# A retention layer's first head: loads in a chain, stores on another queue, sample updates between the two halves of the state

## The chip, the core and the metric

The kernel runs on one core of one Trainium2 chip. The metric is the device time of one launch in microseconds (us). Engines have these names in the profile: PE (matrix products), ACT and DVE (elementwise work), POOL, and SP, which here only issues transfers (DMA). ACT and POOL issue transfers as well. Each engine works through its own queue of instructions in order, and waits at an instruction until the semaphores that it names have been raised.

## The reference, cut to what matters

One inference step of a decoder of two layers: a short gated convolution with its feed-forward part, then a retention layer with its feed-forward part, for 512 prompt tokens and 8 x 4 sample tokens that go on from a stored state. D = 1024, 4 heads, 256 columns of q and k and 512 of v a head. What the change touches is the retention layer:

```python
z = x @ w_in                                     # q, k, v, g of all heads
q = rotary(q, pos); k = rotary(k, pos) * (HEAD_DK ** -0.5)
# per head, in chunks (prompt) or in one step on the stored state s0 (sample):
scores = einsum('bhid,bhjd->bhij', qc, kc) * decay
inner  = einsum('bhij,bhjv->bhiv', scores, vc)
cross  = einsum('bhid,bhdv->bhiv', qc, S) * cross_w
S_new  = S * chunk_decay + einsum('bhjd,bhjv->bhdv', kc * state_w, vc)
# o = inner + cross, normalized per head, times silu(g), then @ w_out
```

The outputs include the new states of prompt and samples. All arithmetic is float32.

## The kernel before

Every product is done in three passes of a reduced float32 type: each operand is split into a high part (rounded, by ACT) and a low part (the rest, by DVE: `split`, L186-188), and high x high, high x low and low x high are summed (`mm3`, `project`, and in the value products L814, L815, L816). So each weight piece is loaded (`load_piece`, L134), split and multiplied. A piece can also be split "adding" (`split_adding`, L189-196): ACT writes the high part and its negative into the place of the low part, and a DMA issued by POOL (L195) adds the weight from memory to it. That spares DVE a pass and costs a transfer that adds.

A scheduler puts instructions into the queues of the engines by the order of the program and by due times; `tc.issue_after(ins)` only keeps an instruction behind `ins` in the same queue. It does not wait for `ins` to be done. Buffers come in turns from pools: a tile that takes the place of others waits for all who still use them.

The retention layer begins inside the feed-forward part of layer 0. `ahead` (L846) makes the q and k of head 0 (L864 scales them, L866 stores them to `qk_made`), the v of head 0 (`value_products(0, ...)`, with `first` None, whose third and fourth weight pieces are loaded inside the loop at L827) and the gates of heads 0 to 2, in six `Job`s (products at L460; `gates`, L888; the store at L906). All of it goes to memory and is loaded again by each head.

Then the heads are walked through in a loop (L1289). For a head but the last:
- `value_products(h + 1, ...)` makes the next head's values from four weight pieces, c0 to c3; L821 is the sample tokens' product with the raw piece. Around the pieces, `first()` calls `value_loaded` (loads `vw` and `vsw`), and `then(c)` loads sample states and makes operands: S0 and S1 after piece 0, S2 and `operands_made` (transposes of k, L1069) after piece 1, `value_sample` after piece 2. For head 0, the loads and rotations of q and k (`qk_loaded`, L971; `gt` is the table of gains, L964; the rotations are L980 and L1011-1016) stand before it.
- `sample_operands`, `value_out` (stores the next head's values), `state(h, 0)` and `state(h, 1)`: the prompt's state after two and four chunks, the first split into `mid` (L187/188).
- `scores` of both halves, then `sample_outputs(0)` (L1231, L1233: the samples' q times the stored state S0), `states_update(0)` (L1249, and on DVE L1254, then the store of S0) and the load of S3 into the place of S0.
- `inner` of four blocks with the other sample outputs and updates between them, the next head's q and k, and `out_project`.

The last head has no next head: two pieces of its gate (`gate_project`) take the place of the values. Their order is written out: `operands_made`, gate 0, `value_sample`, S2, `sample_operands`, `state(0)`, gate 1, `state(1)`.

Of the kernel before, what the change touches and what calls it, by code (L numbers as in the profile page):

```python
# [12 lines left out]
P = 128  # L13
# [6 lines left out]
T = SEQ + NS  # L20
# [28 lines left out]
def hybrid_decode_kernel(ctx: ExitStack, tc: tile.TileContext, a: dict, o: dict):  # L49
# [7 lines left out]
    def nm(s):  # L57
        uid[0] += 1
        return f"{s}_{uid[0]}"
# [71 lines left out]
    def parts2(n, pool=None, tags=("wh", "wl")):  # L131
        return [(pool or wts).tile([P, n], F32R, tag=t, name=nm(t)) for t in tags]

    def load_piece(src, n, parts=False, sw=None, keep=None, adding=False):  # L134

        if sw is None:
            w = wts.tile([P, n], F32, tag="w", name=nm("w"))
            wh, wl = parts2(n)
        else:
            w = sw.tile([P, n], F32, tag="w2", name=nm("w2"))  # L140
            wh, wl = parts2(n, sw, ("h2", "l2"))

        def load(c=slice(0, n), queue=nc.sync):
            last_load[0] = queue.dma_start(w[:, c], src[:, c])

        def parted(c=slice(0, n)):
            if adding:
                return split_adding(wh, wl, w, src)
            return split(wh[:, c], wl[:, c], w[:, c])

        if keep is not None:
            keep.append(w)
        if parts:
            return wh, wl, load, parted
        load()
        parted()
        return wh, wl
# [632 lines left out]
    v_made = [dram.tile([P, 5, DV], F32, tag=f"v{h}", name=nm("vm")) for h in range(NH)]  # L790
    gate_made = [dram.tile([P, 4, T], F32, tag=f"g{h}", name=nm("gm")) for h in range(AHEAD)]

    def value_piece(h, c, raw, adding=False):
        return load_piece(a["rtv"][h, c], 2 * DV, keep=raw, adding=adding)

    def value_products(h, xs, first=None, then=None, ws=None):

        pv = [bank() for _ in range(4)]
        pvs = psum()
        if ws is None:  # L800
            raw = []
            ws = [value_piece(h, c, raw, first is None) for c in range(2)]
        else:
            ws, raw = ws
        if first is not None:
            first()
        for c in range(4):
            wh, wl = ws[c]
            for k2 in range(2):
                kt = 2 * c + k2  # L810
                cw = slice(k2 * DV, (k2 + 1) * DV)
                for tt in range(4):
                    ts_, out = slice(tt * P, (tt + 1) * P), pv[tt]
                    nc.tensor.matmul(out, xh[kt][:, ts_], wh[:, cw], start=(kt == 0), stop=False)  # L814
                    nc.tensor.matmul(out, xh[kt][:, ts_], wl[:, cw], start=False, stop=False)  # L815
                    nc.tensor.matmul(out, xl[kt][:, ts_], wh[:, cw], start=False, stop=(kt == KT - 1))  # L816
            if c % 2:

                for g in range(4):
                    kt = 2 * c - 2 + g  # L820
                    nc.tensor.matmul(  # L821
                        pvs[g * NS : (g + 1) * NS, 0, :], xs[:, kt, :],
                        raw[kt // 2][:, kt % 2 * DV : (kt % 2 + 1) * DV],
                        start=(c == 1), stop=(c == 3), skip_group_check=True,
                    )
            if c < 2:
                ws.append(value_piece(h, c + 2, raw, first is None))  # L827
            if then is not None:
                then(c)
        return pv, pvs  # L830
# [15 lines left out]
    def ahead(tp, fp, sw, one):  # L846
# [16 lines left out]
        def off(which, dt, pt):  # L863
            each(lambda p, d, r: nc.vector.tensor_mul(d, p, r), pt, halves(made[which][:, dt, :]), R)  # L864
            if dt:
                nc.gpsimd.dma_start(qk_made[which], made[which])  # L866

        off(1, 0, pts[0])
        off(1, 1, pts[1])
# [18 lines left out]
        def gates(h, n):  # L888
            made = {}

            def tile2():
                if not made:
                    made[0] = tp.tile([P, 2, T], F32, tag="gu", name=nm("gate"))
                return made[0]

            def gate(what, src):
                g = tile2()
                if what == "c21":
                    nc.scalar.activation(g[:, 1, :HT], src, AF.Silu)
                elif what == "c22":  # L900
                    nc.scalar.activation(g[:, 1, HT:], g[:, 1, HT:], AF.Silu)
                elif what == "c12":
                    nc.scalar.activation(g[:, 0, :], g[:, 0, :], AF.Silu)
                    for i in range(2):
                        nc.scalar.activation(g[:, i, :], g[:, i, :], AF.Copy, scale=g_ret(h * 4 + n + i))
                    nc.scalar.dma_start(gate_made[h][:, n : n + 2, :], g)  # L906

            return Job([a["rtg"][h, n + i] for i in range(2)], oh, ol, sw, summed(tile2, gate))
# [11 lines left out]
    with ExitStack() as c2:  # L920
# [49 lines left out]

        def qk_loaded(st):  # L971

            for which in (1, 0):
                nc.sync.dma_start(st["rot"][which], qk_made[which])
                if which:
                    for i, t in enumerate((cos, sin)):
                        nc.sync.dma_start(t, a["rope"][i])
            for which in (1, 0):
                r = st["rot"][which]
                nc.vector.tensor_mul(r, r, st["gt"][:, which, :].unsqueeze(1).to_broadcast([P, 2, T]))  # L980
                rotate(st, which)
# [43 lines left out]
        def value_loaded(h, st):  # L1025
# [1 line left out]
            vw = tp.tile([P, 4, T], F32, tag="gate", name=nm("vw"), bufs=1)[:, :, :DV]  # L1027
            vsw = tp.tile([P, DV], F32, tag="yn", name=nm("vsw"))
            nc.sync.dma_start(vw, v_made[h][:, 0:4, :])
            nc.sync.dma_start(vsw, v_made[h][:, 4, :])  # L1030
            vh = tp.tile([P, 4, DV], F32R, tag="vyh", name=nm("vh"), bufs=1)
            vl = tp.tile([P, 4, DV], F32R, tag="vyl", name=nm("vl"), bufs=1)
            for i in range(2):
# [186 lines left out]
        def states_load(h, st, i):  # L1220
            r, dt = RD[i]
            S = st["S"][i] = sp.tile([P, 4, DV], F32, tag="S", name=nm("S"))
            nc.sync.dma_start(S, rets_in[r, h, dt])
# [33 lines left out]
        def out_project(h, st, rest=None):  # L1257
# [27 lines left out]
                        residual(n, pts[n])  # L1285
            wide("m")

        st = qk_start(0)
        qk_loaded(st)  # L1289
        for h in range(NH):  # L1290
# [2 lines left out]

            def first():
                value_loaded(h, st)

            def then(c):
                if c == 0:
                    for i in range(2):
                        states_load(h, st, i)  # L1300
                elif c == 1:
                    states_load(h, st, 2)
                    operands_made(h, st)
                elif c == 2:
                    value_sample(h, st)

            if more:
# [6 lines left out]
                outs = [None, (slice(0, 2), va), (2, vb[0]), (3, vb[1]), (4, vc)]  # L1314
                value_out(h + 1, pv, pvs, list(zip(rows, outs)))
                state(h, st, 0)
                state(h, st, 1)
            else:
                gw = load_piece(a["rtg"][h, 0], KT * P)
                first()  # L1320
                for i in range(2):
                    states_load(h, st, i)
                operands_made(h, st)
                gate_project(h, st, 0, ws=gw)
                value_sample(h, st)
                states_load(h, st, 2)
                sample_operands(h, st)
                state(h, st, 0)
                gate_project(h, st, 1)
                state(h, st, 1)  # L1330
            for c in range(2):
                scores(h, st, c)
            sample_outputs(h, st, 0)
            states_update(h, st, 0)
            states_load(h, st, 3)
            yn0 = normalized(inner(h, st, 0))
            sample_outputs(h, st, 1)
            yn1 = normalized(inner(h, st, 1))
# [165 lines left out]
```

## Time and profile before

| | |
|---|---|
| median of 3 runs | 1494.57 us (1493.96 to 1496.03) |
| the profiled execution | 1492.83 us, span 1491.0 us |
| granted clock of PE, mean | 0.991 |
| PE busy | 1458.5 us (98%), 10944 products |
| DVE, ACT, POOL busy | 960.0, 612.1, 90.8 us |
| the six gate jobs' products (L460) | 635.98 to about 700 us |
| first L821 in the pass of head 0, 1, 2 | 710.68, 828.93, 930.29 us |
| first L1207 in the pass of the last head | 1021.83 us |

Times in the trace are counted from the span's start. The profiled execution is 1.8 us longer than its span, and 1.7 us shorter than the median. The clock column of a stretch is the share of full speed that PE was granted; a wait line names PE's tile and line, who ended the wait, the total in us, how often, and the longest. In a timeline line, the last bracket is the engine's idle time before the instruction and who ended it. A DMA line's own time is only that of issuing; the landing is a time of its own.

### The profile page before, as it was taken

Reading aid. Unit: us, or ns where it says so; the run is one execution under the profiler, and the core shown is the slowest. Engines: PE = TensorE matmul, PEld = TensorE weight load, DVE = VectorE, ACT = ScalarE, POOL = GpSimd, SP = SyncE. Lnnn points to the kernel's source line nnn. Section 1 sums busy time; section 2 is a strip of 40 time slices with the busy share of each in tenths; the row PEclk is TensorE's granted clock in tenths of the full one; section 3 lists DMA queues with packets and bytes.
Section 4 is the critical chain, followed back from the end, with each engine's and each line's share of the span. In section 5 each row is a group of like instructions: output and inputs, shape, how many; then the busy total and the mean of one; then the engine's idle time right before and its main releaser. Section 6 shows DMA issues by size and latency. Waiting matters only on the chain.

```text
span 1491.0 us, 26121 instructions
## 1 busy us (share of the span) xinstructions
PE 1458.5 (98%) x10944; PEld 1382.4 (93%) x10944; DVE 960.0 (64%) x1465; ACT 612.1 (41%) x883; POOL 90.8 (6%) x115
## 2 busy tenths in 40 slices
PE   9999999999999999899799999999999999999998
PEld 9999999999999999699479789788799999999997
DVE  6554439848658556675677485594759857848645
ACT  5222365525435335465323312323255625525424
POOL 1000220000000003000000000000030000000002
PEclk9999999999999999899899999999999999999999
DMA  6222273322222316544755573672545232222322
GB/s 222 86 86 86 95 177 106 103 89 100 89 96 96 103 47 167 161 147 156 282 200 184 175 259 122 209 257 72 198 127 128 88 107 90 97 89 100 99 65 82
DMA packets 77591, 195.40 MB, mean 131 GB/s; under 512 B 7184, under 2 KB 24464, under 8 KB 77088
## 3 DMA queue, kind: packets, MB, share of 16 engines
q1 hardware_dynamic: 69984, 171.71, 34.3%
q0 software_dynamic: 3344, 12.20, 4.5%
q10 hardware_dynamic: 4144, 9.81, 1.7%
q8 instruction: 86, 1.41, 0.4%
q14 instruction: 33, 0.27, 0.1%
HBM read 162.82 MB, written 30.88 MB: 130 GB/s over the span
## 4 chain that ended last, share of the span: by engine, by line
PE 88%; DVE 5%; issue 3%; DMA 2%; ACT 1%; POOL 1%; SPq 0%; DVEq 0%; ACTq 0%; POOLq 0%
PE mm L174 35%; PE sm L460 30%; PE sm L174 12%; PE sm L815 2%; PE sm L816 1%; PE sm L814 1%; PE sm L162 1%; DVE S L1254 1%; PE sm L164 1%; PE sm L163 1%; PE sm L1233 1%; DVE wl L188 1%; DMA S<-in_rets_dram 1%; DMA wl<-in_rtv_dram 1%; DVE xl L200 0%
## 5 line engine op out<-in xcount | busy, mean ns | idle before, releaser
L187 ACT ACTIVATE wh<-w 128x1024 fp32r<-128x1024 f32 (+4 forms) x209 | 203.9, 978 | 408.7 <-PE mm L174 204.4
L188 DVE TENSOR_TENSOR wl<-w,wh 128x1024 fp32r<-128x1024 f32 (+4 forms) x209 | 235.8, 1131 | 45.0 <-ACT wh L187 42.8
L460 PE MATMUL sm<-oh,wh 128*128 128x272 f32 x672 | 194.3, 289 | 0.0
L460 PE MATMUL sm<-oh,wl 128*128 128x272 f32 x672 | 194.2, 289 | 0.0
L460 PE MATMUL sm<-ol,wh 128*128 128x272 f32 x672 | 193.9, 289 | 0.0
L174 PE MATMUL mm<-xh,wh 128*128 128x272 f32 x868 | 182.3, 291 | 0.5 <-ACT wh L187 0.3
L174 PE MATMUL mm<-xh,wl 128*128 128x272 f32 x868 | 179.5, 289 | 0.0
L174 PE MATMUL mm<-xl,wh 128*128 128x272 f32 x868 | 178.8, 287 | 0.0
L268 DVE TENSOR_TENSOR x<-x,mm 128x544 f32<-128x544 f32 x85 | 61.2, 720 | 143.5 <-PE mm L174 143.4
L460 PE MATMUL sm<-oh,l 128*128 128x272 f32 x504 | 145.7, 289 | 0.0
L460 PE MATMUL sm<-oh,h 128*128 128x272 f32 x504 | 145.5, 289 | 0.0
L460 PE MATMUL sm<-ol,h 128*128 128x272 f32 x504 | 145.5, 289 | 0.0
L174 PEld LDWEIGHTS mm<-xh,wh 128*128 128x128 f32 x868 | 135.5, 188 | 2.5 <-ACT oh L187 0.8
L174 PEld LDWEIGHTS mm<-xl,wh 128*128 128x128 f32 x868 | 135.9, 188 | 0.1
L174 PEld LDWEIGHTS mm<-xh,wl 128*128 128x128 f32 x868 | 135.3, 188 | 0.6 <-DVE wl L188 0.2
L460 PEld LDWEIGHTS sm<-oh,wh 128*128 128x128 f32 x672 | 126.7, 189 | 0.7 <-ACT u L517 0.4
L460 PEld LDWEIGHTS sm<-oh,wl 128*128 128x128 f32 x672 | 126.8, 189 | 0.0
L460 PEld LDWEIGHTS sm<-ol,wh 128*128 128x128 f32 x672 | 126.6, 188 | 0.0
L188 DVE TENSOR_TENSOR l<-w,h 128x1024 fp32r<-128x1024 f32 x84 | 80.3, 956 | 57.4 <-ACT h L187 57.0
L174 PE MATMUL mm<-xh,f 128*128 128x272 f32 x576 | 99.3, 288 | 0.0
L460 PEld LDWEIGHTS sm<-ol,h 128*128 128x128 f32 x504 | 95.0, 188 | 0.0
L460 PEld LDWEIGHTS sm<-oh,l 128*128 128x128 f32 x504 | 95.0, 188 | 0.0
(284 smaller groups left out, 2999.6 us busy)
## 6 DMA issues: line engine op xcount, KB each, us to landing
w<-in_ffgu_dram SPq DMA_DIRECT2D x88, 512.0 KB, 3.5
w<-in_ffdn_dram SPq DMA_DIRECT2D x96, 192.0 KB, 2.5
S<-in_rets_dram SPq DMA_DIRECT2D x16, 1024.0 KB, 7.9
out_rets_dram<-S SPq DMA_DIRECT2D x16, 1024.0 KB, 4.8
w<-in_cvin_dram SPq DMA_DIRECT2D x21, 512.0 KB, 3.5
w<-in_rtqk_dram SPq DMA_DIRECT2D x16, 512.0 KB, 4.4
w<-in_rtv_dram SPq DMA_DIRECT2D x16, 512.0 KB, 3.9
w<-in_rtg_dram SPq DMA_DIRECT2D x16, 512.0 KB, 3.8
```

The source lines that it names most:

```text
L162: nc.tensor.matmul(out, lh, rh, start=start, stop=False, skip_group_check=True)
L163: nc.tensor.matmul(out, lh, rl, start=False, stop=False, skip_group_check=True)
L164: last_product[0] = nc.tensor.matmul(out, ll, rh, start=False, stop=stop, skip_group_check=True)
L174: last_product[0] = nc.tensor.matmul(half(pt, hf)[:, :HT], w[:, c], act[k][:, hf * HT : (hf + 1) * HT], start=(first and k == ks[0] and i ...
L187: h = nc.scalar.activation(dh, src, AF.Copy)
L188: nc.vector.tensor_sub(dl, src, dh.bitcast(F32))
L268: last_residual[0] = nc.vector.tensor_add(xk, xk, p)
L460: nc.tensor.matmul(out, w[:, c], b[k][:, at, :], start=(first and k == 0 and i == 0), stop=(k == n - 1 and i == 2), skip_group_check=True,)
L814: nc.tensor.matmul(out, xh[kt][:, ts_], wh[:, cw], start=(kt == 0), stop=False)
L815: nc.tensor.matmul(out, xh[kt][:, ts_], wl[:, cw], start=False, stop=False)
L816: nc.tensor.matmul(out, xl[kt][:, ts_], wh[:, cw], start=False, stop=(kt == KT - 1))
L1233: last_product[0] = nc.tensor.matmul(st["po"][32 * g : 32 * g + 8, :], qm[:, dt, g, r, :], st["S"][i][:, g, :], start=False, stop=(i == 3) ...
```

## The change

Six things:
1. In `ahead`, the fourth value piece is no longer split "adding" (`first is None and c == 0`); the other three still are.
2. The two stores of the made q and k (L866) are issued by SP in place of POOL.
3. The last gate job's tile is taken from pool `fp` ("f") in place of `tp` ("gu").
4. Head 0's loads are chained in SP's order: `gt`, k, the cosine and sine tables, q, `vw`, `vsw`, then the third value piece (c2), and behind its load the states S0 and S1. Before, c2, S0 and S1 came ahead of `gt`.
5. In all heads, `sample_outputs(0)`, `states_update(0)` and the load of S3 stand between `state(0)` and `state(1)` (`first_outputs`).
6. In the last head, the first two gate products stand before and right behind `operands_made`.

The number of products is the same. Behind the first hunk, line numbers of the changed kernel differ from those above by one or two.

```diff
--- before.py
+++ after.py
@@ -131,7 +131,7 @@
     def parts2(n, pool=None, tags=("wh", "wl")):
         return [(pool or wts).tile([P, n], F32R, tag=t, name=nm(t)) for t in tags]
 
-    def load_piece(src, n, parts=False, sw=None, keep=None, adding=False):
+    def load_piece(src, n, parts=False, sw=None, keep=None, adding=False, after=None):
 
         if sw is None:
             w = wts.tile([P, n], F32, tag="w", name=nm("w"))
@@ -141,7 +141,8 @@
             wh, wl = parts2(n, sw, ("h2", "l2"))
 
         def load(c=slice(0, n), queue=nc.sync):
-            last_load[0] = queue.dma_start(w[:, c], src[:, c])
+            with tc.issue_after(after.ins) if after is not None else ExitStack():
+                last_load[0] = queue.dma_start(w[:, c], src[:, c])
 
         def parted(c=slice(0, n)):
             if adding:
@@ -790,8 +791,8 @@
     v_made = [dram.tile([P, 5, DV], F32, tag=f"v{h}", name=nm("vm")) for h in range(NH)]
     gate_made = [dram.tile([P, 4, T], F32, tag=f"g{h}", name=nm("gm")) for h in range(AHEAD)]
 
-    def value_piece(h, c, raw, adding=False):
-        return load_piece(a["rtv"][h, c], 2 * DV, keep=raw, adding=adding)
+    def value_piece(h, c, raw, adding=False, after=None):
+        return load_piece(a["rtv"][h, c], 2 * DV, keep=raw, adding=adding, after=after)
 
     def value_products(h, xs, first=None, then=None, ws=None):
 
@@ -802,8 +803,7 @@
             ws = [value_piece(h, c, raw, first is None) for c in range(2)]
         else:
             ws, raw = ws
-        if first is not None:
-            first()
+        after = first() if first is not None else None
         for c in range(4):
             wh, wl = ws[c]
             for k2 in range(2):
@@ -824,7 +824,7 @@
                         start=(c == 1), stop=(c == 3), skip_group_check=True,
                     )
             if c < 2:
-                ws.append(value_piece(h, c + 2, raw, first is None))
+                ws.append(value_piece(h, c + 2, raw, first is None and c == 0, after=after if c == 0 else None))
             if then is not None:
                 then(c)
         return pv, pvs
@@ -863,7 +863,7 @@
         def off(which, dt, pt):
             each(lambda p, d, r: nc.vector.tensor_mul(d, p, r), pt, halves(made[which][:, dt, :]), R)
             if dt:
-                nc.gpsimd.dma_start(qk_made[which], made[which])
+                nc.sync.dma_start(qk_made[which], made[which])
 
         off(1, 0, pts[0])
         off(1, 1, pts[1])
@@ -890,7 +890,8 @@
 
             def tile2():
                 if not made:
-                    made[0] = tp.tile([P, 2, T], F32, tag="gu", name=nm("gate"))
+                    last = h == AHEAD - 1 and n
+                    made[0] = (fp if last else tp).tile([P, 2, T], F32, tag="f" if last else "gu", name=nm("gate"))
                 return made[0]
 
             def gate(what, src):
@@ -970,11 +971,9 @@
 
         def qk_loaded(st):
 
-            for which in (1, 0):
-                nc.sync.dma_start(st["rot"][which], qk_made[which])
-                if which:
-                    for i, t in enumerate((cos, sin)):
-                        nc.sync.dma_start(t, a["rope"][i])
+            loads = [(st["rot"][1], qk_made[1]), (cos, a["rope"][0]), (sin, a["rope"][1]), (st["rot"][0], qk_made[0])]
+            for t, src in loads:
+                last = nc.sync.dma_start(t, src)
             for which in (1, 0):
                 r = st["rot"][which]
                 nc.vector.tensor_mul(r, r, st["gt"][:, which, :].unsqueeze(1).to_broadcast([P, 2, T]))
@@ -1027,7 +1026,7 @@
             vw = tp.tile([P, 4, T], F32, tag="gate", name=nm("vw"), bufs=1)[:, :, :DV]
             vsw = tp.tile([P, DV], F32, tag="yn", name=nm("vsw"))
             nc.sync.dma_start(vw, v_made[h][:, 0:4, :])
-            nc.sync.dma_start(vsw, v_made[h][:, 4, :])
+            st["loaded"] = nc.sync.dma_start(vsw, v_made[h][:, 4, :])
             vh = tp.tile([P, 4, DV], F32R, tag="vyh", name=nm("vh"), bufs=1)
             vl = tp.tile([P, 4, DV], F32R, tag="vyl", name=nm("vl"), bufs=1)
             for i in range(2):
@@ -1285,6 +1284,11 @@
                         residual(n, pts[n])
             wide("m")
 
+        def first_outputs(h, st):
+            sample_outputs(h, st, 0)
+            states_update(h, st, 0)
+            states_load(h, st, 3)
+
         st = qk_start(0)
         qk_loaded(st)
         for h in range(NH):
@@ -1293,11 +1297,13 @@
 
             def first():
                 value_loaded(h, st)
+                return st["loaded"] if h == 0 else None
 
             def then(c):
                 if c == 0:
-                    for i in range(2):
-                        states_load(h, st, i)
+                    with tc.issue_after(last_load[0].ins) if h == 0 else ExitStack():
+                        for i in range(2):
+                            states_load(h, st, i)
                 elif c == 1:
                     states_load(h, st, 2)
                     operands_made(h, st)
@@ -1314,25 +1320,24 @@
                 outs = [None, (slice(0, 2), va), (2, vb[0]), (3, vb[1]), (4, vc)]
                 value_out(h + 1, pv, pvs, list(zip(rows, outs)))
                 state(h, st, 0)
+                first_outputs(h, st)
                 state(h, st, 1)
             else:
                 gw = load_piece(a["rtg"][h, 0], KT * P)
                 first()
                 for i in range(2):
                     states_load(h, st, i)
+                gate_project(h, st, 0, ws=gw)
                 operands_made(h, st)
-                gate_project(h, st, 0, ws=gw)
+                gate_project(h, st, 1)
                 value_sample(h, st)
                 states_load(h, st, 2)
                 sample_operands(h, st)
                 state(h, st, 0)
-                gate_project(h, st, 1)
+                first_outputs(h, st)
                 state(h, st, 1)
             for c in range(2):
                 scores(h, st, c)
-            sample_outputs(h, st, 0)
-            states_update(h, st, 0)
-            states_load(h, st, 3)
             yn0 = normalized(inner(h, st, 0))
             sample_outputs(h, st, 1)
             yn1 = normalized(inner(h, st, 1))
```

## The prediction, made before the changed kernel was run

> **What bounds the kernel now.** I read the page first: which engine fills the span, and what the chain that ended last is made of.
> ```profile
> span 1491.0 us, 26121 instructions
> ...
> PE 1458.5 (98%) x10944; PEld 1382.4 (93%) x10944; DVE 960.0 (64%) x1465; ACT 612.1 (41%) x883; POOL 90.8 (6%) x115
> ...
> PE 88%; DVE 5%; issue 3%; DMA 2%; ACT 1%; POOL 1%; SPq 0%; DVEq 0%; ACTq 0%; POOLq 0%
> ```
> PE is the bound. The change removes no product from it, so it can save only what PE idles (about 25 us inside the span) and what PE's slow clock costs after idling. So the second view is PE's waits:
> ```profile
> PE sm L815 <- DMA wl<-in_rtv_dram: 7.5, 1, 7.5
> PE mm L821 <- DMA w<-in_rtv_dram: 4.2, 1, 4.2
> PE sm L815 <- DVE wl L188: 2.0, 1, 2.0
> PE sm L162 <- ACT vb L835: 1.5, 1, 1.5
> PE sm L1233 <- DMA S<-in_rets_dram: 1.4, 1, 1.4
> PE sm L162 <- ACT knh L187: 1.3, 2, 0.6
> ```
> The 7.5 lies at 615.59-623.04, in the values of head 0 (stage `ahead`). The 4.2, 2.0 and 1.5, half of the 1.3 and 1.2 us of smaller waits lie at 718.54-746.86, in head 0's own pass. The 1.4 is at 973.92, in head 2. Third, a table of stretches (PE busy first, then the weight loads, DVE, ACT and POOL; after them the granted clock, the DMA share and GB/s):
> ```profile
> 615.60:623.04 7.44, 0.00 (x0) 0.00 (x0) 2.93 (x7) 2.25 (x4) 0.86 (x1) 0.68 0.95 234
> 623.04:628.50 5.46, 5.46 (x13) 4.30 (x14) 5.46 (x8) 2.17 (x3) 0.00 (x0) 0.50 0.55 147
> 718.50:722.70 4.20, 0.04 (x2) 0.01 (x1) 4.20 (x7) 1.87 (x2) 0.00 (x0) 0.76 1.03 382
> 722.70:730.40 7.70, 4.63 (x12) 1.73 (x12) 7.70 (x11) 3.08 (x4) 0.00 (x0) 0.50 0.76 268
> ```
> After each long wait the clock is 0.50 for some 5 us: 512-column products then start every 0.427 us instead of 0.234. Last, the timelines of POOL, SP and DVE, for who ends the two long waits:
> ```profile
> 614.43 0.86 POOL L195 DMA_DIRECT2D wl<-in_rtv_dram  x1 [15.42 <-ACT wl L194]
> 615.92 0.86 POOL L195 DMA_DIRECT2D wl<-in_rtqk_dram  x1 [0.64 <-ACT wl L194]
> ```
> ```profile
> 700.29 0.94 SPq L1223 DMA_DIRECT2D S<-in_rets_dram  x2
> 710.62 0.34 SPq L964 DMA_DIRECT2D gt<-in_gtab_dram  x1
> ```
> ```profile
> 716.77 1.29 DVE L980 TENSOR_TENSOR rot<-rot,gt 128x1088 f32<-128x1088 f32 x1 [13.64 <-issue]
> 729.19 1.23 DVE L188 TENSOR_TENSOR wl<-w,wh 128x1024 fp32r<-128x1024 f32 x1
> ```
> The first long wait is an adding DMA, issued at 614.43, landed at 623.00. In head 0 the order on SP is S0 and S1 (1 MB each), then `gt`, which waits for the last gate's store: issued at 702.84, it shares the engines with the two S loads and lands at 710.53. DVE starts the rotations at 716.77 and only then splits the last value piece (729.19), for which PE waits until 730.47.
>
> **Part A, `ahead`: the fourth value piece no longer adds.** ACT and DVE split it like any piece. ACT takes 1.06 us (611.17-612.2), DVE is busy with `ol` until 612.87 and then takes 1.23: the low part is there at 614.1, before PE reaches it (615.59 in the old order). The 7.45 us and the slow clock behind it go. What is late next is the adding DMA of the last q weight: 615.92 to 627.42 (11.5 us) before, while two adding DMAs and three loads shared the engines. It is now issued at about 614.4, one adding DMA fewer beside it. Rows of this form: 5.3 and 5.45 us alone, 6.6 and 6.8 in company, 8.57 and 11.5 crowded. I take 6.0: landed at 620.4. The last q products, which began at 630.47, begin there; they take 5.50: 625.9. Before the split that job 0 needs, DVE now has L864 (0.72) and `ol` (0.72) and then the split (1.22): job 0 starts at 628.3 instead of 635.98, **-7.7 us**. With 5.3 it is -8.3, with 8.57 -5.1, with 11.5 -2.2.
>
> The q/k stores move from POOL to SP. The first finds SP idle. The second makes SP wait for L864 at about 626.9, and behind it are job 1's second weight load (627.82 before) and every later load. Job 1's split then ends at 635.8, and PE needs it at 635.6-635.9: nothing, up to +2.
>
> **Part B, head 0.** S0 and S1 now stand behind c2's load, which stands behind `vsw`. The last gate's store has the engines to itself: the gate store before it took 2.68 us (693.18-695.86), so it lands at 705.5. The changed program's `gt` load still names that store in its waits, in spite of the other tile, so `gt` goes at 705.6, 5.0 earlier. Landings behind it keep their distances: the rotated k and q at 711.5 and 712.9, `vw` at 715.6, `vsw` at 716.3, c2 at 717.6. The price is c2: before, it was there early and its 24 products filled 711.7-717.5. Now PE runs dry at 711.75, and the split of c2 stands where that of c3 stood on DVE, behind both rotations: PE goes on at 730.47 - 5.0 = 725.5, with c3's 24 products still to do. From there to the next head's q/k products, by rows of this head: rest of c2 7.0 (12 of its 20 products at 0.427, 8 at 0.234), transposes 0.8, c3 5.6, small products 1.5, first state half with the placing 3.6, first sample outputs and update 2.25, scores 1.43, further outputs 1.2, second state half 2.8, scores 1.43, a wait for `sl` behind three weight splits on DVE 0.6, two inner blocks, update and outputs 5.9: 34.1 us, so 759.6 instead of 761.62, **-2.0 us**. c3's products now cover the waits for knh, knl and vb (2.9 us before). Ends: if the store still takes its 7.7 us, +3; if the clock is up again at once, -5.
>
> Here the row is 5 us at half clock after a long wait. [...]
>
> **Part C, first sample updates ahead of the second state half.** The store of S0 and the load of S3 behind it go out some 6 us earlier. In head 2 that load was issued at 964.60, landed at 973.88 and cost 1.42: **-1.4 us**. In head 1 it landed at 871.06 for use at 871.10, so it cost nothing. DVE's two updates (1.21 each) now stand ahead of or between the two splits of `mid` (0.64 each), which the second inner half needs and whose banks the second state half needs. Beside them PE has scores and outputs: 0 in heads 1 and 2, up to +1 each.
>
> **Part D, last head.** The 48 gate products move ahead of the transposes, the next 48 between transposes and state. The old waits (0.57 for x, 1.00 for s, 0.63 for knh) are covered, but on ACT the gate's silu and scaling (0.64 and 0.75) now stand ahead of s and knh, and on DVE the gate product ahead of ss: I get 0.6 + 1.3 before knh, and 0.6 behind state(0). Net 0, from -1.5 to +1.5.
>
> **Sum:** -7.7 - 2.0 - 1.4 = -11.1 us. The profiled execution took 1492.83 us (its span 1491.0, 1.8 around it), so 1481.7; the median shown, 1494.57, is 1.7 above that execution, so **1483.5**.
>
> **Rivals.**
> (1) The adding DMA of the last q weight is the next bound: it takes 8.57 to 11.5 us as in the crowd before. For it: the store of `vs`, two gate loads and the value stores are still there. Against it: half a megabyte less. A falls to 2-5: about 1488. Chance 0.17.
> (2) Head 0's chain returns what it takes: the store is no faster, or c2 lands late. Each us later costs one; B is +3 instead of -2: about 1488.5. For it: PE is dry from 711.75 and nothing else can fill it. Chance 0.15.
> (3) Slower: the first updates hold up the second state half. Place: `mid` behind two L1254 on DVE, in four heads. A head's price is at most 2 x 1.21 + 2 x 0.64 = 3.7, plus what S0's load is late for its earlier use. It decides from (11.1 + 3) / 4 = 3.5 us a head, uncovered; at 4 us a head the time is 1499.5. Against it: PE's scores and outputs lie between, and S0 of heads 1 to 3 had been loaded long before. Chance 0.08.
> (4) The change does not do what it says: the moved tile frees nothing, and the fourth piece's split is late by the `ol` ahead of it on DVE, so the stall stays in part; A and B near 0: 1493, within 0.2% of before. Chance 0.05.
> Forecast: chance 0.55.
>
> **How the numbers follow.** A measurement can tell about 0.2%, 3 us, from no change, so faster is below 1491.6 and slower above 1497.6. Forecast, (1) and (2) are faster, unless (1) and (2) meet with the costs of the other parts (1491 and more): 0.85 of the 0.87 that they hold. (4) and that remainder give "same" 0.07, (3) 0.08. The range goes from all parts at their good ends (-8.3 - 5 - 1.4 - 1.5 = -16.2: 1478.4, and 3 below for waits that I did not count) to (1) and (2) together (1483.5 + 2.6 + 5 = 1491.1): 1476 to 1492.
>
> **What would show it.** Right: no wait for `wl<-in_rtv_dram` at L815 and a clock of 1.00 there; job 0's L460 some 7-8 us earlier; `gt` issued 5 us earlier against the end of the gates; PE idle in head 0 still near 10 us, but in one place, waiting at L821 for c2 and at L815 for DVE; no wait for S in head 2. Wrong: a wait for `wl<-in_rtqk_dram` over 3 us in `ahead`, `gt` still issued 8 us behind the store, PE waits for `mid` over 1 us in a head.

## The result and the profile after

| | before | after |
|---|---|---|
| median | 1493.36 us (1490.94 to 1496.03) | 1490.08 us (1488.49 to 1491.61) |
| ratio, 95% interval | | 0.9976 (0.9966 to 0.9986) |
| profiled execution, span | 1492.83, 1491.0 us | 1488.64, 1486.8 us |
| granted clock of PE, mean | 0.991 | 0.994 |
| PE idle up to its last product | 25.5 us | 15.2 us |
| PE's last product ends | 1483.92 us | 1479.52 us |

Both kernels have nine runs here. By the ratio the change makes the kernel 3.6 us faster (2.1 to 5.1); 1483.5 had been predicted, and 1490.1 lies near the upper end of the range. The question of the study is therefore where about 7 of the 11.1 us forecast went. First the page of after:
```profile
span 1486.8 us, 26122 instructions
...
PE 1464.4 (98%) x10944; PEld 1384.0 (93%) x10944; DVE 960.4 (65%) x1466; ACT 611.1 (41%) x882; POOL 90.0 (6%) x112
...
PE 92%; DVE 3%; ACT 1%; issue 1%; DMA 1%; POOL 0%; DVEq 0%; SPq 0%; ACTq 0%; POOLq 0%
```
PE idles 10.3 us less. But its busy time has risen from 1458.5 to 1464.4 us with the same 10944 products: 5.9 us come back as busy time. The PE waits (tile and line, releaser, total, count, longest; line numbers are one higher than before):
```profile
PE mm L821 <- DMA w<-in_rtv_dram: 5.2, 1, 5.2
PE mm L175 <- ACT wh L188: 2.8, 3, 0.9
...
PE sm L461 <- ACT wh L188: 1.1, 1, 1.1
```
The 7.5 us of the adding DMA, the 2.0 of DVE's `wl` and the 1.4 of S are gone. The 5.2 is the one long wait in head 0, at 707.1 to 712.3. New are three waits of 0.9 at L175, one in each of heads 0, 1 and 2, and 1.1 at the first product of job 0. The stretches of after (busy time of PE, weight loads, DVE, ACT, POOL, then granted clock, DMA share, GB/s):
```profile
620.90:627.10 6.20, 6.20 (x51) 5.99 (x48) 4.13 (x6) 2.43 (x5) 0.00 (x0) 1.00 0.90 298
627.10:630.00 2.90, 1.34 (x8) 1.03 (x8) 2.90 (x5) 2.90 (x5) 0.00 (x0) 1.00 0.68 277
630.00:633.40 3.40, 3.40 (x18) 3.40 (x17) 3.23 (x5) 1.19 (x4) 0.00 (x0) 0.52 0.55 196
707.10:712.30 5.20, 0.02 (x4) 0.00 (x0) 5.20 (x8) 1.85 (x2) 0.00 (x0) 0.97 1.04 396
712.30:718.70 6.40, 5.91 (x12) 1.68 (x12) 6.40 (x9) 3.11 (x4) 0.00 (x0) 0.50 0.86 324
```
In `ahead`, PE no longer stands still at 615.6 to 623.0, and it is busy at full clock up to 627.1; then come two short waits and 3.4 us at half clock. In head 0 the long wait, and the slow clock behind it (0.50), remain. Two DMA issues of after, from the timelines of POOL and SP:
```profile
614.78 0.87 POOL L196 DMA_DIRECT2D wl<-in_rtqk_dram  x1 [15.57 <-ACT wl L195]
```
```profile
700.39 0.33 SPq L965 DMA_DIRECT2D gt<-in_gtab_dram  x1
```
The adding DMA of the last q weight lands at 620.73, 5.95 us after its issue. `gt` is issued 2.77 us behind the last gate's store (697.62); before it was 7.78.

The times at which stages start on PE give the balance:

| stage | before | after | difference |
|---|---|---|---|
| job 0's first product | 635.82 | 628.24 | -7.58 |
| the gate jobs, first to last product | 64.15 | 67.11 | +2.96 |
| head 0, first sample product of c0/c1 to that of head 1 | 118.18 | 116.19 | -1.99 |
| head 1, likewise | 101.36 | 103.12 | +1.76 |
| head 2, last head and the rest | 553.70 | 554.15 | +0.45 |
| sum, from the start to the last product | | | -4.40 |

Two things hide in the three lower rows.

**Groups that are cut.** A sample output (L1232) is four products of 8 columns, each on its own 32 rows of the output, and each product is two records. In head 1, the PE timelines of before and of after show them so:
```profile
854.46 1.05 PE L1233 MATMUL sm<-S,qm 128*8 128x512 f32 x8
856.76 1.04 PE L1233 MATMUL sm<-S,qm 128*8 128x512 f32 x8
859.77 1.04 PE L1233 MATMUL sm<-S,qm 128*8 128x512 f32 x8
```
```profile
845.21 1.02 PE L1232 MATMUL sm<-S,qm 128*8 128x512 f32 x2
851.26 1.04 PE L1232 MATMUL sm<-S,qm 128*8 128x512 f32 x6
854.26 1.04 PE L1232 MATMUL sm<-S,qm 128*8 128x512 f32 x8
```
Before, all eight records of a group stand together: the four products start within 0.02 us and the group holds PE for 0.98 us. After, the scheduler has put the first product of S1's group ahead of `state(1)` (845.21) and the other three 6 us later. The one alone holds PE for 0.95 us, the three for 0.97: a cut costs 0.95 us. There are four cuts, S2's in head 0 and S1's in heads 1, 2 and 3. Taken from the start of each of these records to the start of PE's next one, they hold PE for 15.61 us before and 19.28 after, +3.67. The mean of a record is 594 ns in both kernels, so the mean does not show it; the total does. From the groups of before and after, 700 to 1100 us:
```profile
L1233 PE MATMUL sm<-S,qm 128*8 128x512 f32 x128 | 16.7, 594 | 1.4 <-DMA S<-in_rets_dram 1.4
```
```profile
L1232 PE MATMUL sm<-S,qm 128*8 128x512 f32 x128 | 20.6, 594 | 0.0
```
So the four products of a group, each on its own 32 rows, hold PE about as long as one of them: 0.98 us for four, 0.95 for one.

**A late last block.** DVE in head 0 of after:
```profile
770.60 1.21 DVE L1253 SCALAR_TENSOR_TENSOR S<-S,mm 128x1024 f32<-128x1024 f32 x1
772.32 0.69 DVE L1159 BATCH_NORM_STATS2 bst<-sm 128x6 f32<-128x512 f32 x1
...
777.66 0.81 DVE L1163 TENSOR_SCALAR yn<-sm,mv,rs 128x512 f32<-128x512 f32 x1
...
780.02 0.68 DVE L1190 TENSOR_TENSOR gate<-gate,mm 128x512 f32<-128x512 f32 x1
```
S3 is loaded earlier, so its updates (L1253) have come to stand ahead of the statistics of the last inner block (L1159). `yn`, the transposes and the product with the gate (L1190) are late by that, and L1190 frees the bank that the next head's q and k products need:
```profile
780.84 0.49 PE L175 MATMUL mm<-xh,wh 128*128 128x272 f32 x2 [0.93 <-ACT wh L188]
```
The bracket names ACT's split `wh`, which ended 780.82. This product does not use that split, whose low part DVE has ready only at 782.46, while PE goes on to the products with the low part at 781.42; in the program it waits for an earlier split, long done, and for DVE's L1190, which ended 780.70. The same wait stands at 883.96 and 987.11: 2.8 us in all.

### The profile page after: what moved, and what is told of

The parts are those of the page before. It is cut to its first block, busy times and chain, and to the rows that moved or that the text cites. A ratio compares the mean times of both kernels' runs of the same rounds, so it can differ in the third digit from the quotient of the medians.

```text
span 1486.8 us, 26122 instructions
## 1 busy us (share of the span) xinstructions
PE 1464.4 (98%) x10944; PEld 1384.0 (93%) x10944; DVE 960.4 (65%) x1466; ACT 611.1 (41%) x882; POOL 90.0 (6%) x112
## 4 chain that ended last, share of the span: by engine, by line
PE 92%; DVE 3%; ACT 1%; issue 1%; DMA 1%; POOL 0%; DVEq 0%; SPq 0%; ACTq 0%; POOLq 0%
PE mm L175 36%; PE sm L461 29%; PE sm L175 13%; PE sm L815 2%; PE sm L816 2%; PE sm L814 2%; PE sm L163 2%; PE sm L164 1%; PE sm L165 1%; PE sm L1232 1%; DVE wl L189 1%; PE mm L821 1%; DMA w<-in_rtg_dram 1%; DVE xl L201 1%; PE mm L1248 0%
## 5 line engine op out<-in xcount | busy, mean ns | idle before, releaser
L175 PE MATMUL mm<-xh,wh 128*128 128x272 f32 x868 | 182.9, 291 | 3.0 <-ACT wh L188 2.8
L175 PE MATMUL mm<-xh,wl 128*128 128x272 f32 x868 | 179.7, 289 | 0.0
L175 PE MATMUL mm<-xl,wh 128*128 128x272 f32 x868 | 179.2, 288 | 0.1
L175 PEld LDWEIGHTS mm<-xh,wh 128*128 128x128 f32 x868 | 135.9, 189 | 5.3 <-ACT wh L188 3.3
L175 PEld LDWEIGHTS mm<-xl,wh 128*128 128x128 f32 x868 | 136.1, 189 | 0.4 <-DVE xl L201 0.3
L175 PEld LDWEIGHTS mm<-xh,wl 128*128 128x128 f32 x868 | 135.5, 189 | 0.6 <-DVE wl L189 0.2
L175 PE MATMUL mm<-xh,f 128*128 128x272 f32 x576 | 99.3, 288 | 0.0
L461 PEld LDWEIGHTS sm<-oh,h 128*128 128x128 f32 x504 | 95.4, 189 | 1.1 <-ACT h L188 0.7
```

The costliest lines, as they stand in the source:

```text
L175: last_product[0] = nc.tensor.matmul(half(pt, hf)[:, :HT], w[:, c], act[k][:, hf * HT : (hf + 1) * HT], start=(first and k == ks[0] and i ...
L461: nc.tensor.matmul(out, w[:, c], b[k][:, at, :], start=(first and k == 0 and i == 0), stop=(k == n - 1 and i == 2), skip_group_check=True,)
```

## Experiments

My theory for the loss was that the cut groups (3.7), the late block (2.8) and the give-back in the gate jobs (3.0) took it. Rivals were that part 5 costs nothing and the chain in head 0 brings nothing, or that the adding DMA or the place of c2 decides. Each ratio is to before in the same session, with its 95% interval; that of after is 0.9976 (0.9966 to 0.9986). A run is called apart from another where the two intervals do not overlap; lengths of stages are those of one execution's trace.

**Part 5 undone** (e1_no_first).
```diff
                 state(h, st, 0)
-                first_outputs(h, st)
                 state(h, st, 1)
...
             for c in range(2):
                 scores(h, st, c)
+            first_outputs(h, st)
```


> The changed kernel with the first sample outputs, update 0 and the load of S3 back behind the scores (part 5 undone, all else kept). Theory 1 (part 5 costs more than it brings: a group of four sample-output products that is cut in 1 + 3 costs 0.95 us each time, four times, one cut staying here in head 0; and a late last block costs a 0.93 us wait of L175 in heads 0, 1 and 2; against 1.4 us saved at the load of S3 in head 2): -2.85 - 2.8 + 1.4 = -4.2, so about 1485.8 us against 1490.1; no wait of 0.93 in a head, the S wait of about 1.4 us in head 2 back. Rival (part 5 is what gains; the lost time is elsewhere): 1.4 us slower, 1491.5.


Measured: 1486.71 us, 0.9936 (0.9923 to 0.9948), apart from after. Only one cut (16.55 us start to start) and one wait of 0.93 are left, both in head 0; the wait for S is back with 1.87 in head 2. In the trace, head 1 takes 101.53 us against 103.12 in after. Another 1.2 us of this trace's gain lie in the gate jobs (65.91 against 67.11), whose clock did not fall here (1.00 from 626 to 636) and which the edit does not touch. So part 5 costs more than the wait that it removes, and head 0's share of cut and late block comes also without it.

**Part 5 alone, on the kernel before** (e4_only_first). `first_outputs` in every head, in the last one ahead of gate 1; nothing else of the change.


> The kernel before with part 5 alone. Theory 1: +3.8 (four cut groups) + 2.8 (three late last blocks) - 1.4 (S3 of head 2) = +5.2, about 1498.6 against 1493.4. Rival (part 5 gains by itself): -1.4, 1492.


Measured: 1498.72 us, 1.0027 (1.0017 to 1.0036), that is +4.0 us. The sample products hold 19.40 us and the three waits are there:
```profile
PE mm L174 <- ACT wh L187: 2.8, 3, 0.9
```
The working was 3.8 + 2.8 - 1.4 = +5.2; the interval, +2.5 to +5.4, takes it in, and leaves the rival's -1.4 out. By stages, head 0 is 1.2 us longer than before (119.37) and head 1 1.8 (103.13).

**Groups held whole, part 5 kept** (e2_whole). The order of the sample outputs is fixed behind the inner blocks.
```diff
             yn0 = normalized(inner(h, st, 0))
-            sample_outputs(h, st, 1)
+            with tc.issue_after(last_product[0].ins):
+                sample_outputs(h, st, 1)
             yn1 = normalized(inner(h, st, 1))
+            inner1 = last_product[0]
             states_update(h, st, 1)
-            sample_outputs(h, st, 2)
+            with tc.issue_after(inner1.ins):
+                sample_outputs(h, st, 2)
```


> The changed kernel with the sample outputs 1 and 2 queued behind the inner block before them, so that PE's order keeps all groups of four together; part 5 stays. Theory 1: 4 x 0.95 = 3.8 us less, about 1486.3, with the three waits of 0.93 us still there, and L1232-type products at 0.12 us mean start-to-start instead of 0.15. Rival (the cut groups cost nothing, their products are short and only spread out): within 0.5 us of 1490.1.


Measured: 1488.64 us, 0.9957 (0.9942 to 0.9972). The products hold 15.61 us again, as before, so the cuts are gone. The time fell by 0.2%, with an interval that overlaps that of after, so what the cuts alone cost in time is not shown; part of what they freed on PE went into waits. Four of its PE waits:
```profile
PE mm L175 <- ACT wh L188: 3.1, 4, 0.9
PE sm L461 <- ACT wh L188: 1.6, 1, 1.6
PE sm L163 <- DVE mid L189: 1.4, 3, 0.8
...
PE sm L175 <- DVE yn L1163: 0.6, 1, 0.6
```
Here the wait for `mid`, which the prediction's rival 3 named, does appear, with 1.4 us in all.

**Part 5 undone and groups whole** (e8_no_first_whole). The edits of the first and the third run together.


> The changed kernel with part 5 undone and the sample outputs 1 and 2 queued behind their inner blocks (no cut group at all). Theory 1: 0.95 us less than with part 5 undone alone (its one cut group, in head 0), and the 0.93 us wait in head 0 stays or goes with DVE's order there: ratio 0.992 to 0.993 against 0.9936. Rival (cut groups cost nothing): 0.9936.


Measured: 1485.64 us, 0.9939 (0.9926 to 0.9951): the same as with part 5 undone alone, within what a measurement can tell, and short of the 0.992 to 0.993 expected. The one cut is gone (15.61), a wait of 0.92 at 779.62 stays. Its stretch behind job 0's start says something else:
```profile
627.90:630.00 2.10, 1.59 (x8) 1.16 (x9) 2.10 (x3) 2.10 (x4) 0.00 (x0) 1.00 0.65 269
630.00:633.40 3.40, 3.40 (x29) 3.40 (x28) 3.28 (x5) 1.11 (x3) 0.00 (x0) 1.00 0.70 181
```
With waits of 1.00 and 0.43 the clock stays at 1.00, and the gate jobs take 65.97 us. In after, with 1.13 and 0.43, it fell (0.52 in the stretch 630.0 to 633.4), with 67.11 us. So of the 2.96 us by which the jobs grew, the slow clock has about 1.1; the rest is there without it.

**Statistics first** (e9_stats). On top of the whole groups, the statistics of the last inner block are taken ahead of the updates of S2 and S3; `normalized` is parted into `stats_of` and its last step.
```diff
                 yn2 = normalized(p2)
+                s3 = stats_of(p3)
...
-                yn3 = normalized(p3)
+                yn3 = normalized(p3, stats=s3)
```


> The changed kernel with part 5 kept, the sample outputs 1 and 2 queued behind their inner blocks, and the mean and variance of the last inner block taken before the updates 2 and 3 in the program. Theory 1, second half (with S3 there early, DVE does updates 2 and 3, 1.2 us each, ahead of the last block's statistics, so that its gate product is late and the next 48 products wait 0.93 us for the bank): the three waits of L175 go, 2.8 us less than e2_whole, ratio 0.9957 - 0.0019 = 0.9938. Rival (those waits are ACT's weight split, as the profile names it): they stay, 0.9957.


Measured: 1486.52 us, 0.9942 (0.9928 to 0.9956), apart from after, though not from the run with whole groups alone. No wait of L175 for `wh` is left in the three heads:
```profile
PE mm L821 <- DMA w<-in_rtv_dram: 4.5, 1, 4.5
PE sm L461 <- ACT wh L188: 1.8, 1, 1.8
PE sm L163 <- DVE mid L189: 1.4, 3, 0.8
...
PE mm L175 <- ACT yh L188: 1.2, 1, 1.2
```
Only DVE's order was changed, and ACT's split of the weight was left where it was: the waits came from DVE, not from the engine that the profile names.

**Part 1 undone: all later value pieces add** (e6_adding).
```diff
-                ws.append(value_piece(h, c + 2, raw, first is None and c == 0, after=after if c == 0 else None))
+                ws.append(value_piece(h, c + 2, raw, first is None, after=after if c == 0 else None))
```


> The changed kernel with part 1 undone: the fourth value piece adds again. If the waits of 1.13 and 0.43 us and the half clock at job 0's start (2.3 us in all, and some 0.5 more in the jobs) are the price of the earlier start, undoing part 1 costs 7.6 - 2.8 = 4.8 us: ratio from 0.9976 to about 1.001, job 0 at full clock from its first product. Rival (job 0's slow start has another cause and stays): 7.6 us, ratio 1.003.


Measured: 1493.8 us, 0.9997 (0.9988 to 1.0006), apart from after. The wait at L815 is back with 6.95 and job 0 starts at 635.23, 7.0 later than in after; but the gate jobs take 64.15 us, at full clock (1.00 at 635 to 641), and the last gate product is only 4.03 later. That is the give-back: of 7.0 us ahead of job 0, 3.0 are lost by the end of the jobs.

**Part 4 undone: no chain in head 0** (e5_unchained). c2, S0 and S1 are loaded as early as before.
```diff
-                ws.append(value_piece(h, c + 2, raw, first is None and c == 0, after=after if c == 0 else None))
+                ws.append(value_piece(h, c + 2, raw, first is None and c == 0))
...
-                    with tc.issue_after(last_load[0].ins) if h == 0 else ExitStack():
+                    with ExitStack():
```


> The changed kernel with part 4 undone: c2, S0 and S1 again ahead of gt in SP's order, all else kept (PE's order has again four cut groups of sample outputs). Theory 3 (the chain is worth what the trace shows for head 0 once the costs of part 5 are set apart: 2.0 us net + 0.93 + 0.95 = 3.9 us): ratio to before up from 0.9976 by 0.0026 to about 1.000. Rival (the prediction's size of that part, 2.0 us): 0.999. Both expect gt to be issued 7 to 8 us behind the last gate's store again instead of 2.8.


Measured: 1492.73 us, 0.9984 (0.9975 to 0.9993), 1.2 above after by the ratios, with overlapping intervals. The trace is clearer: head 0 takes 119.39 us against 116.19, and the wait of 2.0 for `wl` is back, and so is one of 0.6 for `knh`. `gt` goes out 7.5 us behind the gate's store again. The chain is worth 3.2 us in the trace; how much of it the time keeps is not settled.

**Parts 2 and 3 undone** (e7_pool_gu): stores of q and k on POOL, the last gate tile in `tp`.
```diff
-                nc.sync.dma_start(qk_made[which], made[which])
+                nc.gpsimd.dma_start(qk_made[which], made[which])
...
-                    last = h == AHEAD - 1 and n
+                    last = False
```


> The changed kernel with parts 2 and 3 undone: the stores of q and k on POOL again, the last gate's tile in the old pool. The prediction had both at 0: ratio 0.9976 unchanged, gt still issued right behind the landing of the last gate's store. Rival (SP waiting for the q/k product holds up job 1's weight load, or the tile's place matters): 1 to 2 us either way, seen as a change of job 1's first product or of the issue of gt.


Measured: 1489.35 us, 0.9961 (0.9949 to 0.9974). Nothing is lost without these parts. `gt` still goes out right behind the gate's store: it is the order on the queue, not the tile, that brings it forward (2.77 us behind the store in after, 7.5 with S0 and S1 loaded ahead of it in the unchained run).

**Sample products of the fourth value piece first** (e3_raw_first), so that their buffers come free earlier for job 0's weights.
```diff
         for c in range(4):
             wh, wl = ws[c]
+            if c == 3 and first is None:
+                sample_products(c)
```


> The changed kernel with the sample products of the fourth value piece ahead of its other products in the stage ahead of the heads, so that the buffer of the raw piece comes free some 5 us earlier and the weight of job 0 is loaded at about 615.5 instead of 621.45. Theory 2 (that late load sets job 0's start: waits of 1.13 and 0.43 us, then 3.4 us at half clock that cost 1.6): up to 3.2 us less, 1486.9 to 1488.5, clock 1.00 at 628 to 634. Rival (DVE's queue, which splits for job 0 until 629.6, sets the start anyway): no change, 1490.


Measured: 1491.42 us, 0.9976 (0.9964 to 0.9988), no change: the rival's number, but not for the rival's reason. Two gate loads go out early (614.41 and 615.49, where after has 620.95 and 621.45), but beside them the adding DMA of the q weight takes 9.7 us (615.07 to 624.75) instead of 5.95:
```profile
PE mm L175 <- DMA wl<-in_rtqk_dram: 4.1, 1, 4.1
```
That is rival 1 of the prediction, brought about by two loads more beside that DMA.

**The same, with the last q weight not adding** (e10_q_split).
```diff
-        qw = load_piece(a["rtqk"][0, 1], KT * P, adding=True)
+        qw = load_piece(a["rtqk"][0, 1], KT * P)
```


> The changed kernel with the sample products of the fourth value piece ahead of its other products, as in e3, and the last q weight split without adding as well. Theory 2 (job 0's start is set by its late weight load; in e3 that load came early but slowed the adding DMA of the q weight, for which PE then waited 4.1 us): no adding DMA is left to wait for, so the waits of 1.13 and 0.43 us shrink and the gate jobs take 64 to 65 us instead of 67: 2 to 3 us less, ratio 0.9976 - 0.0017 = 0.996. Rival (DVE's queue sets the start: one more split of 1.2 us on it makes job 0 later): 0.998 or more.


Measured: 1486.61 us, 0.9942 (0.9930 to 0.9955), apart from after. Job 0 starts at 625.98, 2.3 us earlier than in after; the jobs take 66.2 us, and not the 64 to 65 expected. The time fell further than either theory said.

**Both together** (e11_no_first_q): part 5 undone and groups whole, and the last two edits.


> e8_no_first_whole together with the two edits of e10: if they add up, 0.9939 - 0.0017 = 0.992; if DVE's queue is the bound at job 0, 0.994.


Measured: 1484.23 us, 0.9928 (0.9916 to 0.9941), between the two.

**Part 5 kept, all repairs** (e12_stats_q): groups whole, statistics first, sample products first, the q weight not adding.


> e9_stats together with the two edits of e10, part 5 kept: if they add up, 0.9938 - 0.0017 = 0.992, and no wait for S in head 2; else 0.994.


Measured: 1481.40 us (1480.58 to 1482.44), 0.9911 (0.9898 to 0.9925). By the ratios this beats both kernels, by 13 us and by some 10. Its page, and its one long PE wait:
```profile
span 1478.7 us, 26115 instructions
```
```profile
PE mm L811 <- DMA w<-in_rtv_dram: 5.4, 1, 5.4
```

**That kernel with c2 loaded early** (e13_c2_early), the chain kept for S0 and S1, to see whether the last long wait can go.
```diff
-                ws.append(value_piece(h, c + 2, raw, first is None and c == 0, after=after if c == 0 else None))
+                ws.append(value_piece(h, c + 2, raw, first is None and c == 0))
...
-                    with tc.issue_after(last_load[0].ins) if h == 0 else ExitStack():
+                    with tc.issue_after(st["loaded"].ins) if h == 0 else ExitStack():
```


> e12_stats_q with c2 loaded early again, ahead of gt, as in the kernel before; S0 and S1 stay behind vsw. If c2 behind vsw is only a price (PE idles 5.4 us at L821 for it), PE has c2's 24 products then: 3 to 5 us less, ratio 0.988 to 0.989. If DVE's rotations set the end in any case, PE only waits later, for c3's split (L815, some 7 us) and for knh, knl and vb (2.9 us before) with no products left to cover them: 1 to 3 us more, 0.992 to 0.993.


Measured: 1479.68 us, 0.9912 (0.9899 to 0.9926), no difference; it lies in the gap between what the two theories expected. Head 0 takes 112.92 us against 114.49, and PE waits for the rotated q in place of c2 (3.43 at 714.81): the profile names no releaser, but on DVE the first half of q's rotation ends at 714.7. The wait has changed its place and is 2 us shorter, but the measured time did not follow.

**The kernel with all repairs and the last head's old order** (e14_old_last; part 6 undone).


> e12_stats_q with the last head's old order (operands, gate 0, state(0), gate 1, then the first outputs and state(1)). The prediction's 0 for that order: ratio 0.991 as e12. Rival (the old waits of 0.57, 1.00 and 0.63 us come back, the new ones of 0.57 and 0.86 go): 0.8 us more.


Measured: 1484.18 us, 0.9945 (0.9932 to 0.9959). The three old waits (0.57, 1.00, 0.63) are back, and the trace from the start of head 2 on is longer by 0.96 us. The difference of 5 us by the ratios is more than that, and so is the traces' own, 3.5; the rest of the latter lies in stretches that this edit does not touch (1.4 ahead of 614 us, 0.5 in head 0, 0.7 in head 1), and why stays open. Part 6 is worth 1.0 us where its trace can be read.

## Why the prediction was right in sign and too large

By its own steps, on the trace (differences in us):

| step | forecast | shown |
|---|---|---|
| A: job 0 earlier | -7.7 | -7.6 |
| A: gate jobs behind it | 0, up to +2 | +3.0 |
| B: head 0 | -2.0 | -2.0 |
| C: head 1 | 0, up to +1 | +1.8 |
| C and D: head 2, last head and the rest | -1.4 | +0.4 |
| sum | -11.1 | -4.4 |

What lies inside the last three rows can only be counted, not read off. Four cuts at 0.95 and three late blocks at 0.93 make +6.6, and the wait for S -1.4; what is left by subtraction is -3.9 for the chain in head 0, -0.1 in head 1 and -1.0 for part D. The runs bear this out only in part: without the chain head 0 is 3.2 us longer, not 3.9, and part 5 alone makes head 0 longer by 1.2, not 1.9.

**Part A: the arrival was right, in part by luck, and its sequel was not.** The adding DMA took 5.95 us (6.0 forecast) and job 0 starts at 628.24 (628.3); before, its first product stands at 635.82, a little ahead of the 635.98 that the forecast counted from. But the path is another: the q products run until 627.1 and not 625.9, and job 0 waits for ACT's `wh` (627.14 to 628.18), not for a split on DVE behind L864. ACT comes to it late because the `oh` ahead of it needs DVE's L407, which stands behind L421, and that waited until 624.55 for a gate load issued at 620.95. The failed step is "nothing, up to +2" for what comes behind. After the wait of 1.13 ahead of job 0, its products wait another 0.43 for a split, with DVE and ACT both busy for the whole of 627.1 to 630.0; then the clock is at half (0.50) for 3.4 us; job 1 waits 0.2. So an earlier start met the same splitting engines, and the jobs stretched by 2.96, some 1.1 of it by the slow clock. The run with all value pieces adding shows the two ends: 7.0 us later at job 0, 4.0 at the last gate product.

**Part B: right mechanism, and a net that agrees by luck.** Head 0 is 2.0 us shorter, as forecast, but as the difference of two terms: the chain brings 3.2 (the run without it), and 1.2 go to a cut group and a late block (the run with part 5 alone), which the forecast did not have. With part 5 undone, head 0 keeps one of each and takes 116.09 us, so the chain alone also nets about 2. The order came as forecast: `gt` goes 5.0 us earlier behind its store, c2 lands 11.8 behind `gt` (12.0 forecast), and the last split behind both rotations, of c2 in place of c3, comes 12.4 us after they begin, in before (716.77 to 729.19) as in after (705.52 to 717.95). The mis-sized terms are small ones: the rotations begin 5.1 us behind `gt`'s issue instead of 6.15, and `gt` itself is 0.6 earlier against PE. So the low part's products go on at 719.22, 12.1 us after PE ran dry, and not 13.75, which more than covers the 1.2. "PE idle near 10 us" was wrong in form: PE waits 5.2 us for c2, and then the products that need no low part, at half clock (0.50), fill most of the rest.

**Part C: the failed step.** I priced it by one wait and by the two updates beside `mid`. The wait went, and `mid` was not waited for by more than 0.2 in after. The price came from where no step looked: DVE's queue at the end of the head, where the updates of the early S3 overtook the last block's statistics, and PE's order, where products with nothing to wait for any more went in singly. The run with part 5 alone (+4.0) and the one without it show the price of part 5 as a whole; how it divides between cuts and late blocks is counted in the traces and not shown in time. Rival 3 had the part and the sign right and the place wrong; its threshold of 3.5 us a head was not reached: by the count heads 0 to 2 paid 1.9 each and the last 0.95, and in head 0 a cut and a late block come with the chain alone.

**Part D** was taken as zero; the covered waits count for 1.0 by subtraction and by the trace of the repaired kernel with the old order.

**The other rivals.** Rival 1 did not occur in after, but its condition is as near as two loads: it did in the run with the sample products first. Rival 2 is refuted by the unchained run's trace. Of rival 4 a part is true: the moved tile frees nothing, at no cost.

**The step common to all:** the sum was one of waits, and took the products' own time and order as fixed. The page of after contradicts that in its second line: PE's busy time rose by 5.9 us, of which the cut groups are 3.7; what is left was not taken apart (the ends of products are modelled).

## What to carry to other kernels

When an edit lets a scheduler start small work earlier, look at the order on the bounding engine, not at its waits alone: products that run side by side are worth holding together (here four held PE for 0.98 us, one alone for 0.95), and PE's busy time at an unchanged count is the line that shows when they aren't. A load that comes earlier brings its followers earlier too; ask for each whom it now overtakes in the queue (here the updates of S3 overtook the statistics, for 2.8 us of waits). And an earlier start is worth only what the engines that feed it can follow (here 3.0 of 7.6 us were lost again by the end of the gate jobs).

## What the runs showed of the hardware

- Four products of 8 columns on different 32-row stripes of the output hold PE for 0.98 us together, one alone for 0.95.
- The clock fell to half (0.50) for 3.4 us after waits of 1.13 and 0.43 within 2 us; in the run with part 5 undone and groups whole, with waits of 1.00 and 0.43, it did not. In after it changes at 630.11, 633.53, 712.03 and 722.27, which are whole multiples of 3.413 us apart. Cut along that grid, after and then the other run (its change at 709.31 gives its grid) differ in this:
```profile
626.70:630.11 3.41, 1.85 (x12) 1.33 (x11) 3.41 (x5) 3.41 (x5) 0.00 (x0) 1.00 0.72 288
630.11:633.53 3.42, 3.42 (x17) 3.42 (x17) 3.25 (x5) 1.21 (x3) 0.00 (x0) 0.50 0.59 200
```
```profile
623.98:627.39 3.41, 3.00 (x25) 2.78 (x23) 2.97 (x6) 1.07 (x2) 0.00 (x0) 1.00 0.92 338
627.39:630.80 3.41, 2.40 (x15) 1.96 (x16) 3.41 (x5) 2.95 (x4) 0.00 (x0) 1.00 0.50 201
```
In after both waits lie in one such stretch, which leaves PE busy for 1.85 us of it and never idle for more than 1.13; in the other run they fall into two, with 3.00 and 2.40. Cut in the same way up to PE's last product, the traces of before and after have four stretches at full clock with a fall behind them, with PE busy for 0.68, 1.23, 1.85 and 0.00 us (from 614.91 and 717.31 in before, 626.70 and 708.62 in after). The least busy ones without a fall have 1.87 (741.20 in before) and 1.91 (705.21 in after); the ends of products are modelled.
- An adding DMA of 512 KB took 5.95 us beside stores and gate loads, and 9.7 us with two more gate loads of 512 KB on the way.
- The releaser that a profile names can be the operation that merely ended last: the run with the statistics first removed three waits of 0.9 us "for ACT" by changing DVE alone.
